# Layer 1's feed-forward part: down products written between block products, and the second half's operands made during the first half and kept in DRAM

## The chip, the cores and the metric

One core of a Trainium2 chip runs the whole program. The metric is the device time of one execution, in microseconds, and the time of a kernel is the median of its runs. Matrix products run on PE (TensorE) in float32; DVE (VectorE), ACT (ScalarE) and POOL (GpSimd) do the elementwise work; SP (SyncE) issues most DMAs, ACT a few. Each engine takes its own instructions strictly in their order, and waits at an instruction until what it needs is there.

## What is computed

The reference is a two-layer transformer block over 1024 latent tokens of width 1024 with a prefix of 256 context tokens. Layer 0 mixes tokens by a Fourier transform and windowed attention, layer 1 by neighbourhood attention over a 64-wide grid; each layer ends in a gated feed-forward part. Only layer 1's feed-forward part is touched, and in the last layer it covers the latent tokens alone:

```python
h = _rms(x, norm2_g[1]) * (1.0 + sc2) + sh2
x = x + g2 * ((silu(h @ wg) * (h @ wu)) @ wd)      # wg, wu: 1024 x 2816, wd: 2816 x 1024
```

## The kernel before

Every float32 operand of a product is split into a high and a low part of fewer bits, and each product is three matmuls: high x high, high x low, low x high (`mm3`, lines 74 to 76).

**Two halves.** Layer 1's feed-forward part runs over the tokens in two halves of 512 (`ci` 0 and 1), and in each over 22 tiles of 128 hidden columns, so over 44 tiles in all. `x` holds the residual stream for all tokens in SBUF.

**Block products ("p").** Gate and up projection of a tile are not multiplied out directly. The two weight blocks and the two halves of the contraction are combined so that 7 products of half size take the place of 8: `product7` (12 matmuls of 128x256 each) multiplies one of seven weight combinations (`t1` to `t4` are sums and differences of raw weight blocks, made on POOL at L1359) by one of seven operand combinations, held for the current half in `c_hi` and `c_lo`. `product` takes the seven results out of PSUM (`p_ps`, 3 buffers) into `p1`, `u2`, `u3`, `av`, `sg`, and at the end splits the tile's activation into `act_hi` (ACT) and `act_lo` (POOL).

**Weights of a block product.** `prepare1` and `parts_of` round a combination to `w_hi` (ACT, L1240), copy it into PSUM (`pmisc`, ACT, L1244, 2 buffers) and subtract it there on DVE to get `w_lo` (L1245); the seventh combination's `w_lo` is made on POOL. `w_hi` and `w_lo` have 6 buffers each.

**Down products ("d").** For each pair of tiles, 8 products of 6 matmuls of 128x512 (`down_product`) go to `d_ps` (PSUM, 3 buffers), and DVE adds each to `x` (L1437). The down weights are loaded as they are (`wd_raw`) and split by ACT (L1387) and POOL (L1388) into space of an earlier buffer, so that the trace shows them as `h_hi` and `h_lo`.

**Order.** The list `items` sets the order in this part, and PE, DVE, ACT and POOL take the instructions as written. Seven block products of a tile stand together, then four down products of the pair before; tiles 0 and 1 of each half have none, and each half ends with 4 + 8 down products in a row. Preparation runs up to 5 products ahead of use, and at most 7 items.

**Between the halves.** `norm1s(1)` normalises the second half during the first: 18 steps, four per tile from tile 1 on, the results stored to DRAM (`h_d`). At the end of the first half they are loaded back, and `combine` (16 half-width adds on POOL, 16 casts on ACT, 16 subtractions on DVE) makes `c_hi` and `c_lo` from them among the last down products.

Of the kernel before, what the change touches and what calls it, by code (L numbers as in the profile page):

```python
# [63 lines left out]
def build(tc, io):  # L64
# [1209 lines left out]
    def norm1s(ci, done):  # L1274


        ts = slice(ci * 512, ci * 512 + 512)
        ss = wk.tile([P, 512], F32, name="nrm_ss")
        for i, k in enumerate(reversed(range(KT))):
            if i == 0:  # L1280
                S.activation(ss, x[:, k, ts], AF.Square)
            else:
                sq = wk.tile([P, 512], F32, name="nrm_sq", **(dict(tag="nrm_r") if ci else dict(tag="t", bufs=4)))
                S.activation(sq, x[:, k, ts], AF.Square)
                G.tensor_tensor(ss, ss, sq, ALU.add)
            yield
        for r in norm_rstd(ss, 512, wk, ph):
            yield
        for i in range(4):
            both = []  # L1290
            for k in (i, i + 4):
                a, b = nA[3][:, k, 0:1], vec(1, 3)[:, k, 0:1]
                if ci:
                    h = wk.tile([P, 512], F32, name="nrm_h", tag="nrm_ss")
                    G.tensor_tensor(h, x[:, k, ts], r, ALU.mult)
                    S.activation(h, h, AF.Identity, bias=b, scale=a)
                    nc.scalar.dma_start(h_d[:, k], h)
                else:
                    t = wk.tile([P, 512], F32, name="nrm_t", tag="t", bufs=4)
                    V.scalar_tensor_tensor(t, x[:, k, ts], a, r, ALU.mult, ALU.mult)  # L1300
                    h = wk.tile([P, 512], F32, name="nrm_h", tag="wd", bufs=4)
                    S.activation(h, t, AF.Identity, bias=b, scale=1.0)
                both.append(h)
                yield
            if not ci:
                done(i, *both)
                yield
# [4 lines left out]
    def combine(i, h0, h4, tags=("act_hi", "act_lo")):  # L1312

        s, r = (wk.tile([P, 2, HT], F32, name="s_sum", tag=t, bufs=4) for t in tags)
# [16 lines left out]

    items = []
    for ci in range(2):
        for f in range(NF):
            items += [("p", ci, f, s) for s in range(7)]
            if f >= 2:
                items += [("d", ci, f // 2 * 2 - 2, dt) for dt in range(f % 2 * 4, f % 2 * 4 + 4)]
        items += [("d", ci, NF - 2, dt) for dt in range(KT)]
    products = [(n, i) for n, i in enumerate(items) if i[0] == "p"]
    LEAD_P, LEAD_I = 5, 7  # L1340
    tiles = {}

    def load_tile(n):

        if n < 2 * NF:
            f = n % NF
            tiles[n] = dict(b=[raw_half(io[w][1, f][:, i:i + 4])
                               for w, i in (("w_gate", 0), ("w_up", 0), ("w_up", 4), ("w_gate", 4))], w={})

    def prepare1(n, s):  # L1350

        if s == 0:
            load_tile(n + 1)
        d = tiles[n]
        b11, b12, b22, b21 = d["b"]

        def weight_sum(name, a, b):
            d[name] = wk.tile([P, 4, P], F32, name=name, tag="t", bufs=4)
            G.tensor_tensor(d[name], a, b, ALU.subtract)  # L1359

        if s == 0:
            weight_sum("t1", b12, b11)
            weight_sum("t2", b22, d["t1"])
        elif s == 1:
            weight_sum("t3", b22, b12)
        elif s == 3:
            weight_sum("t4", d["t2"], b21)
        src = (b11, d["t2"], d.get("t3"), d["t1"], d.get("t4"), b21, b22)[s]
        d["w"][s] = parts_of(src, G if s == 6 else V)
# [4 lines left out]
    h_d = tc.dram_tile([P, KT, 512], F32, name="h_d")  # L1374
    down_raw = {}

    def load_down(n):
        for h in range(2):
            raw = wk.tile([P, 4, P], F32, name="wd_raw", tag="wd", bufs=4)
            nc.sync.dma_start(raw, io["w_down"][1, n % NF][:, 4 * h:4 * h + 4])  # L1380
            down_raw[n, h] = raw

    def split_down(n, h):
        f = n % NF
        hi, lo = (w_room[f // 2 % 2][:, f % 2, h, t] for t in range(2))
        raw = down_raw.pop((n, h))
        S.copy(hi, raw)  # L1387
        G.tensor_tensor(lo, raw, fl(hi), ALU.subtract)  # L1388

    later = {}  # L1390

    def product(i, n, s):

        d = tiles[n]
        if s == 0:
            for name in ("p1", "u2", "u3", "sg"):
                d[name] = wk.tile([P, HT], F32, name=name)
            d["av"] = wk.tile([P, 2, HT], F32, name="av", bufs=2)
            d["act"] = [wk.tile([P, 512], F32R, name=m, bufs=4) for m in ("act_hi", "act_lo")]
        p1, u2, u3, sg, av, (hi, lo) = (d[k] for k in ("p1", "u2", "u3", "sg", "av", "act"))  # L1400
        ps = product7(d["w"].pop(s), (0, 4, 5, 3, 2, 1, 6)[s])
# [20 lines left out]
        else:  # L1422
# [3 lines left out]
            after(2, lambda: S.copy(hi, avf))  # L1426
            after(3, lambda: G.tensor_tensor(lo, avf, fl(hi), ALU.subtract))

    def down_product(ci, n, dt):
        f = n % NF  # L1430
        w_in = w_room[f // 2 % 2]
# [9 lines left out]
    own0 = norm1s(0, combine)  # L1441
# [5 lines left out]
    own1 = norm1s(1, None)  # L1447
    def first_tile():
        load_tile(0)
        for s in range(LEAD_P):  # L1450
            prepare1(0, s)
# [3 lines left out]
    done_p = LEAD_P  # L1455
    h_in = []
    with tc.manual_schedule(engines={E.PE, E.DVE, E.Activation, E.Pool}):
        now_p = 0
        for i, (kind, ci, f, s) in enumerate(items):
            n = ci * NF + f  # L1460
            while done_p < len(products) and done_p < now_p + LEAD_P + 1 and products[done_p][0] <= i + LEAD_I:
                _, pc, pf, ps_ = products[done_p][1]
                prepare1(pc * NF + pf, ps_)
                done_p += 1
            for step in later.pop(i, ()):
                step()
            if kind == "p":
                product(i, n, s)
                now_p += 1
                if s == 3:  # L1470
                    load_down(n)
                if f and s in (2, 5):
                    split_down(n - 1, s // 5)
            else:
                down_product(ci, n, s)
                last = i + 12 >= len(items) or items[min(i + 12, len(items) - 1)][1] > ci

                rest = sum(1 for it in items[i:i + 12] if it[0] == "d" and it[1] == ci) if last else 13
                if last and rest in (12, 10):
                    split_down(ci * NF + NF - 1, 0 if rest == 12 else 1)  # L1480
                if last and ci == 0 and rest in (11, 8, 5, 2):
                    j = (11 - rest) // 3
                    combine(j, *h_in[j], tags=("t", "t"))
            if ci == 0 and kind == "p" and f and s % 2 == 0:
                advance(own1, 1)
            if ci == 0 and kind == "p" and f == NF - 1 and s == 6:

                rooms = [dict(tag="nrm_ss"), dict(tag="nrm_r")], *([dict(tag="wd", bufs=4)] * 2,) * 3
                for k, room in enumerate(rooms):
# [121 lines left out]
```

## Time and profile before

| | |
|---|---|
| median of 3 runs | 2988.53 us (2986.49 to 2993.25) |
| the profiled execution's own time | 2990.69 us |
| its span in the trace | 2988.9 us |
| PE busy | 2821.1 us, 94% of the span |
| DVE, ACT, POOL busy | 51%, 41%, 27% |
| layer 1's feed-forward part | from 2198 us to the end |

The span runs from the first to the last instruction; the 1.8 us between it and the execution's own time lie around it. An idle time in the trace is put down to the event that came last before the engine went on, its releaser. `pmisc` and `p_ps` are PSUM buffers, `w_raw` and `wd_raw` raw weights.

### The profile page before, as it was taken

The page shows a single profiled execution, that of the slowest core. Times are in us where ns is not written, and L with a number is a line of the kernel's source. Part 1 is how long each engine was busy: PE and PEld are TensorE (multiplying, and loading weights), DVE is VectorE, ACT ScalarE, POOL GpSimd, SP SyncE. Part 2 cuts the span into 40 slices and gives each one's busy share as a digit, 9 for nine tenths or more (in the row PEclk, how much of TensorE's full clock was granted, in tenths as well). Part 3 has the DMA queues.
Part 4 walks back from the last instruction along what each step waited for, and adds up shares of the span by engine and source line. Part 5 has one row for each costly group of instructions (what it writes and reads, how often), then busy time and mean ns, then how long its engine had stood idle before and what let it go on. Part 6 is the DMA issues. An engine that isn't in the chain of part 4 may idle for free. (4 is left out here: it accounts for less than half of the span.)

```text
span 2988.9 us, 44472 instructions
## 1 busy us (share of the span) xinstructions
PE 2821.1 (94%) x16874; PEld 2352.6 (79%) x16874; DVE 1515.3 (51%) x3085; ACT 1212.9 (41%) x2402; POOL 810.4 (27%) x841
## 2 busy tenths in 40 slices
PE   7989999999999999999989999999986999889999
PEld 5876768888888888888767887777776888778888
DVE  5775553622323333333575242666464666656665
ACT  4345552511111111111353232666365666466664
POOL 1112332000000000000220003554155666656664
PEclk9989999999999999999999999999998999999999
DMA  7236664111011111011134236873542322332321
GB/s 273 81 119 232 213 213 139 57 43 36 29 50 43 36 36 43 29 43 43 56 113 144 84 103 173 192 180 86 170 136 86 110 95 99 103 106 96 99 97 68
DMA packets 154982, 310.60 MB, mean 104 GB/s; under 512 B 13424, under 2 KB 71280, under 8 KB 147728
## 3 DMA queue, kind: packets, MB, share of 16 engines
q1 hardware_dynamic: 146336, 288.80, 30.6%
q0 software_dynamic: 1952, 8.32, 1.0%
q10 hardware_dynamic: 6480, 10.63, 0.9%
q8 instruction: 133, 2.18, 0.3%
q14 instruction: 81, 0.66, 0.1%
HBM read 264.58 MB, written 43.12 MB: 103 GB/s over the span
## 5 line engine op out<-in xcount | busy, mean ns | idle before, releaser
L74 PE MATMUL p_ps<-c_hi,w_hi 128*128 128x256 f32 x1232 | 346.7, 281 | 17.5 <-DVE u L1414 7.3
L76 PE MATMUL p_ps<-c_hi,w_lo 128*128 128x256 f32 x1232 | 345.3, 280 | 2.0 <-DVE w_lo L1245 1.9
L75 PE MATMUL p_ps<-c_lo,w_hi 128*128 128x256 f32 x1232 | 345.5, 280 | 0.0
L810 POOL TENSOR_TENSOR nrm_ss<-nrm_ss,nrm_sq 128x512 f32<-128x512 f32 (+1 forms) x31 | 39.3, 1268 | 1013.2 <-PE d_ps L76 935.7
L775 ACT CAST w_hi<-w_raw 128x1024 fp32r<-128x1024 f32 x106 | 110.3, 1049 | 482.6 <-PE d_ps L75 270.5
L74 PEld LDWEIGHTS p_ps<-c_hi,w_hi 128*128 128x128 f32 x1232 | 236.4, 192 | 21.4 <-ACT pmisc L1244 6.9
L76 PEld LDWEIGHTS p_ps<-c_hi,w_lo 128*128 128x128 f32 x1232 | 236.1, 192 | 2.4 <-DVE w_lo L1245 2.4
L75 PEld LDWEIGHTS p_ps<-c_lo,w_hi 128*128 128x128 f32 x1232 | 236.1, 192 | 2.1 <-DVE c_lo L1322 0.2
L580 POOL TENSOR_SCALAR pr<-pr,st 128x640 f32<-128x640 f32 (+2 forms) x208 | 156.0, 751 | 267.4 <-DVE st L579 177.0
L878 DVE SCALAR_TENSOR_TENSOR x<-d_ps,mod,x 128x512 f32<-128x512 f32 (+1 forms) x240 | 157.4, 660 | 125.4 <-PE d_ps L76 125.4
L776 DVE TENSOR_TENSOR w_lo<-w_raw,w_hi 128x1024 fp32r<-128x1024 f32 x102 | 124.1, 1223 | 183.7 <-ACT w_hi L775 181.4
L862 DVE TENSOR_TENSOR sg<-sg,u_ps 128x512 f32<-128x512 f32 (+1 forms) x66 | 39.5, 598 | 320.2 <-PE u_ps L76 320.2
L1245 DVE TENSOR_TENSOR w_lo<-t,pmisc 128x512 fp32r<-128x512 f32 x176 | 119.7, 680 | 150.8 <-ACT pmisc L1244 145.3
L74 PE MATMUL d_ps<-act_hi,w_hi 128*128 128x512 f32 (+1 forms) x528 | 189.4, 359 | 3.4 <-DVE x L878 3.4
L75 PE MATMUL d_ps<-act_lo,w_hi 128*128 128x512 f32 (+1 forms) x528 | 189.2, 358 | 1.3 <-DVE act_lo L864 1.3
L76 PE MATMUL d_ps<-act_hi,w_lo 128*128 128x512 f32 (+1 forms) x528 | 189.3, 359 | 0.0
L74 PE MATMUL u_ps<-o_hi,w_hi 128*128 128x512 f32 (+1 forms) x528 | 188.4, 357 | 0.0
L76 PE MATMUL u_ps<-o_hi,w_lo 128*128 128x512 f32 (+1 forms) x528 | 188.4, 357 | 0.0
L75 PE MATMUL u_ps<-o_lo,w_hi 128*128 128x512 f32 (+1 forms) x528 | 188.4, 357 | 0.0
L74 PE MATMUL g_ps<-o_hi,w_hi 128*128 128x512 f32 (+1 forms) x528 | 188.4, 357 | 0.0
L76 PE MATMUL g_ps<-o_hi,w_lo 128*128 128x512 f32 (+1 forms) x528 | 188.3, 357 | 0.0
L75 PE MATMUL g_ps<-o_lo,w_hi 128*128 128x512 f32 (+1 forms) x528 | 188.3, 357 | 0.0
(328 smaller groups left out, 7478.7 us busy)
## 6 DMA issues: line engine op xcount, KB each, us to landing
ada_w<-ada_w SPq DMA_DIRECT2D x48, 1024.0 KB, 4.9
wd_raw<-w_down SPq DMA_DIRECT2D x88, 256.0 KB, 2.8
w_raw<-w_gate SPq DMA_DIRECT2D x88, 256.0 KB, 2.6
w_raw<-w_up SPq DMA_DIRECT2D x88, 256.0 KB, 2.7
k<-k_d SPq DMA_DIRECT2D x28, 640.0 KB, 10.3
w_raw<-w_in SPq DMA_DIRECT2D x24, 512.0 KB, 4.2
w_raw<-w_gate SPq DMA_DIRECT2D x22, 512.0 KB, 3.4
w_raw<-w_up SPq DMA_DIRECT2D x22, 512.0 KB, 3.5
```

The source lines that it names most:

```text
L74: TE.matmul(out, lh, rh, start=first, stop=False)
L75: TE.matmul(out, lh, rl, start=False, stop=False)
L76: TE.matmul(out, ll, rh, start=False, stop=last)
L580: G.tensor_scalar(self.pr[:, :n], self.pr[:, :n], st[:, 3:4], 0.0, ALU.mult, ALU.add)
L775: S.copy(hi, raw)
L776: eng.tensor_tensor(lo, raw, fl(hi), ALU.subtract)
L810: adder(i).tensor_tensor(ss, ss, sq, ALU.add)
L862: V.tensor_tensor(sg[:, :n], sg[:, :n], u_ps[:, :n], ALU.mult)
L878: V.scalar_tensor_tensor(xs, self.shaped(ps[:, :n]), vec(l, 5)[:, dt, v:v + 1], xs, ALU.mult, ALU.add)
L1245: eng.tensor_tensor(lo, src, first, ALU.subtract)
```

## The change

The feed-forward part's work is written in another order, and the second half's operands are made elsewhere:

- `items` puts the four down products of a tile after its third, fifth, sixth and seventh block product, one after each; for tile 22 (the first of the second half) all four stand after the second block product. Tiles now count through from 0 to 43, so that a pair's down products may fall into the next half.
- Preparation is three functions with fixed leads: `sums1` (POOL) 7 products ahead, `high1` (ACT) 5, `low1` 4.
- Splitting the down weights is four steps at four products of a tile, where it was two.
- `norm1s` makes the complete `c_hi` and `c_lo` of the second half during the first: normalise, combine, round, subtract, all on POOL and ACT, in 58 steps of which four stand in each tile from tile 1 on. It stores the parts to DRAM (`c_d`) with 32 DMAs issued by ACT. In tile 21, after each block product, two DMAs on SP load the operand that this product was the last to read. `combine` is used for the first half only.
- `act_hi` and `act_lo` have 3 buffers instead of 4, `wd_raw` has 3 of its own.

```diff
+    def norm1s():
...
+        for i in range(4):
+            h0, h4, s_, r_ = (wk.tile([P, 512], F32, name="own", bufs=4) for _ in range(4))
+            for k, h in ((i, h0), (i + 4, h4)):
+                G.tensor_tensor(h, x[:, k, 512:], r, ALU.mult)
+                S.activation(h, h, AF.Identity, bias=vec(1, 3)[:, k, 0:1], scale=nA[3][:, k, 0:1])
                 yield
+            G.tensor_tensor(s_[:, M1], h0[:, M2], h4[:, M2], ALU.add)
+            G.tensor_tensor(s_[:, M2], s_[:, M1], h0[:, M1], ALU.subtract)
+            yield
+            G.tensor_tensor(r_[:, M1], h0[:, M1], h0[:, M2], ALU.subtract)
+            G.tensor_tensor(r_[:, M2], h4[:, M1], s_[:, M2], ALU.subtract)
+            yield
+            for sl, src in ((slice(0, 1), h0[:, M1]), (slice(1, 3), h4), (slice(3, 5), s_), (slice(5, 7), r_)):
+                n = (sl.stop - sl.start) * HT
+                hi = wk.tile([P, 512], F32R, name="own_hi", tag="nrm_ss")
+                S.copy(hi[:, :n], src)
+                G.tensor_tensor(src.bitcast(F32R), src, fl(hi[:, :n]), ALU.subtract)
+                yield
+                for t, part in ((0, fl(hi[:, :n])), (1, src)):
+                    nc.scalar.dma_start(c_d[:, sl, t, i], part.rearrange("p (a n) -> p a n", n=HT))
+                yield
...
-    for ci in range(2):
-        for f in range(NF):
-            items += [("p", ci, f, s) for s in range(7)]
-            if f >= 2:
-                items += [("d", ci, f // 2 * 2 - 2, dt) for dt in range(f % 2 * 4, f % 2 * 4 + 4)]
-        items += [("d", ci, NF - 2, dt) for dt in range(KT)]
+    for n in range(NT1):
+        downs = [("d", n // 2 * 2 - 2, dt) for dt in range(n % 2 * 4, n % 2 * 4 + 4)] if n > 1 else []
+        where = (2, 4, 5, 6)
+        if n == NF:
+            where = (1, 1, 1, 1)
+        for s in range(7):
+            items.append(("p", n, s))
+            items += [d for d, w in zip(downs, where) if w == s]
+    items += [("d", NT1 - 2, dt) for dt in range(KT)]
...
-        for i, (kind, ci, f, s) in enumerate(items):
-            n = ci * NF + f
-            while done_p < len(products) and done_p < now_p + LEAD_P + 1 and products[done_p][0] <= i + LEAD_I:
-                _, pc, pf, ps_ = products[done_p][1]
-                prepare1(pc * NF + pf, ps_)
-                done_p += 1
+        for i, (kind, n, s) in enumerate(items):
             for step in later.pop(i, ()):
                 step()
...
+            q = 7 * n + s
+            sums1(q + LEAD + 2)
+            if q:
+                low1(q + LEAD - 1)
+            high1(q + LEAD)
+            product(i, n, s)
...
+            if 0 < n < NF - 1 and s in (0, 2, 4, 6):
                 advance(own1, 1)
-            if ci == 0 and kind == "p" and f == NF - 1 and s == 6:
...
+            if n == NF - 1:
 
+                for t, dst in ((0, c_hi), (1, c_lo)):
+                    nc.sync.dma_start(fl(dst[:, SLOTS[s]]), c_d[:, SLOTS[s], t])
```

What this makes of the engines' queues shows at three places.

DVE, one tile of the first half well after its start. Before, from the last block product's `u` on, all four additions to `x` stand behind it, with two further `w_lo` among them:

```order
L1419 TENSOR_TENSOR sg<-p_ps,p_22244 128x256
L1245 TENSOR_TENSOR w_lo<-t_22350,pmisc 128x512
L1421 TENSOR_TENSOR av<-av,u_22246 128x256
L1424 TENSOR_TENSOR u_22245<-p_ps,u_22245 128x256
L1245 TENSOR_TENSOR w_lo<-t_22326,pmisc 128x512
L1425 TENSOR_TENSOR av<-u_22245,sg 128x256
L1437 SCALAR_TENSOR_TENSOR x<-d_ps,mod_72,x 128x512
L1245 TENSOR_TENSOR w_lo<-t_22397,pmisc 128x512
L1437 SCALAR_TENSOR_TENSOR x<-d_ps,mod_72,x 128x512
L1245 TENSOR_TENSOR w_lo<-w_raw,pmisc 128x512
L1437 SCALAR_TENSOR_TENSOR x<-d_ps,mod_72,x 128x512 x2
```

DVE of the changed kernel, the same part of a tile:

```order
L1475 TENSOR_TENSOR u_22136<-u_22136,p_ps 128x256
L1505 SCALAR_TENSOR_TENSOR x<-d_ps,mod_72,x 128x512
L1425 TENSOR_TENSOR w_lo<-t_22178,pmisc 128x512
L1478 TENSOR_TENSOR sg<-p_ps,p_22134 128x256
L1480 TENSOR_TENSOR av<-av,u_22136 128x256
L1505 SCALAR_TENSOR_TENSOR x<-d_ps,mod_72,x 128x512
L1425 TENSOR_TENSOR w_lo<-t_22126,pmisc 128x512
L1483 TENSOR_TENSOR u_22135<-p_ps,u_22135 128x256
L1484 TENSOR_TENSOR av<-u_22135,sg 128x256
L1505 SCALAR_TENSOR_TENSOR x<-d_ps,mod_72,x 128x512
```

Each `x` now stands right behind the block product that its down product follows on PE, and one `w_lo` between two of them.

POOL, one tile of the first half while the second half is being normalised. Before (`nrm_h` is the second half's normalised operand, `h_lo` a split of down weights):

```order
L1359 TENSOR_TENSOR t_19590<-w_raw 128x512
L1359 TENSOR_TENSOR t_19592<-w_raw,t_19590 128x512
L1295 TENSOR_TENSOR nrm_h<-x,nrm_r 128x512
L1359 TENSOR_TENSOR t_19618<-w_raw 128x512
L1388 TENSOR_TENSOR h_lo<-wd_raw,h_lo 128x512
```

POOL of the changed kernel, one tile later (`own` holds the second half's operands, `own_hi` their high parts):

```order
L1340 TENSOR_TENSOR own<-own,own_hi 128x256
L1400 TENSOR_TENSOR t_19940<-w_raw 128x512
L1340 TENSOR_TENSOR own<-own,own_hi 128x512
L1492 TENSOR_TENSOR act_lo<-av,act_hi 128x512
L1400 TENSOR_TENSOR t_19971<-w_raw,t_19940 128x512
L1446 TENSOR_TENSOR h_hi<-wd_raw,h_hi 128x512
L1400 TENSOR_TENSOR t_19992<-w_raw 128x512
L1425 TENSOR_TENSOR w_lo<-w_raw,w_hi 128x512
```

The sums for the next tile now stand two products ahead of the cast that reads them, and subtractions for `own` have come between them.

SP at the turn of the halves. Before, the stored `h_d` comes back in eight loads behind the last weights of the first half:

```order
L1233 DMA w_raw<-h_d 128x512 x2
L1380 DMA wd_raw<-w_down 128x512
L1233 DMA w_raw<-h_d 128x512 x2
L1494 DMA h_in<-h_d 128x512 x2
L1380 DMA wd_raw<-w_down 128x512 x2
```

SP of the changed kernel, in tile 21:

```order
L1554 DMA c_lo<-c_d 128x1024
L1554 DMA c_hi<-c_d 128x1024 x2
L1554 DMA c_lo<-c_d 128x1024
L1233 DMA w_raw<-w_up 128x512
L1233 DMA w_raw<-w_gate 128x512
L1554 DMA c_hi<-c_d 128x1024
L1554 DMA c_lo<-c_d 128x1024
```

Fourteen loads of twice the size stand there now, the first two operands' ahead of two of the four weight loads of tile 23.

199 lines of the change are left out of this document (112 added, 87 removed).

## The prediction

> **What bounds the kernel now.** I read the share of PE first (94% of the span), then the busy times by stretch of the changed part, then the moment at which ACT takes each tile's first block product out of PSUM, which clocks the tiles, and last what PE waits for.
>
> ```profile
> span 2988.9 us, 44472 instructions
> PE 2821.1 (94%) x16874; PEld 2352.6 (79%) x16874; DVE 1515.3 (51%) x3085; ACT 1212.9 (41%) x2402; POOL 810.4 (27%) x841
> ...
> 2205.45:2331.59 126.14, 91.67 (x594) 84.12 (x595) 58.26 (x112) 76.90 (x138) 77.16 (x61) 0.86 0.29 97
> 2331.59:2575.07 243.48, 230.70 (x1622) 209.57 (x1621) 156.14 (x286) 151.56 (x286) 152.92 (x120) 1.00 0.30 98
> 2684.20:2960.16 275.96, 261.49 (x1838) 237.48 (x1837) 176.84 (x324) 171.81 (x323) 173.25 (x136) 1.00 0.28 92
> ...
> L74 PE MATMUL p_ps<-c_hi,w_hi x1232: 275/276/582, 2198.3 to 2967.8; 128*128 128x256 f32 x176
> ```
>
> The stretches give length, then busy time (and instructions) of PE, PE's weight loads, DVE, ACT and POOL, then granted clock, DMA share and GB/s. The last row is the first of a block product's three matmuls: the part begins at 2198.3. No engine but PE is busy for more than two thirds of a steady stretch, yet PE idles in all three. The tiles' clock, ACT's copy out of `p_ps`, for tiles 0, 6, 7, 21, 22, 26 and 43:
>
> ```profile
> 2205.45 0.36 ACT L1407 COPY p<-p_ps 128x256 f32<-128x256 f32 x1
> 2331.59 0.37 ACT L1407 COPY p<-p_ps 128x256 f32<-128x256 f32 x1 [1.99 <-PE p_ps L76]
> 2347.82 0.37 ACT L1407 COPY p<-p_ps 128x256 f32<-128x256 f32 x1 [1.99 <-PE p_ps L76]
> 2575.07 0.37 ACT L1407 COPY p<-p_ps 128x256 f32<-128x256 f32 x1 [1.99 <-PE p_ps L76]
> 2621.97 0.37 ACT L1407 COPY p<-p_ps 128x256 f32<-128x256 f32 x1 [1.96 <-PE p_ps L74]
> 2684.20 0.37 ACT L1407 COPY p<-p_ps 128x256 f32<-128x256 f32 x1 [1.99 <-PE p_ps L76]
> 2960.16 0.37 ACT L1407 COPY p<-p_ps 128x256 f32<-128x256 f32 x1 [1.99 <-PE p_ps L76]
> ```
>
> What PE's own work takes: a tile's seven block products, from their first matmul to the first down product, and two additions to `x` at the end, where DVE only follows PE:
>
> ```profile
> 2715.09 0.28 PE L74 MATMUL p_ps<-c_hi,w_hi 128*128 128x256 f32 x1
> 2724.62 0.39 PE L74 MATMUL d_ps<-act_hi,h_hi 128*128 128x512 f32 x1
> 2983.71 0.75 DVE L1437 SCALAR_TENSOR_TENSOR x<-d_ps,mod,x 128x512 f32<-128x512 f32 x1 [0.65 <-PE d_ps L76]
> 2985.11 0.75 DVE L1437 SCALAR_TENSOR_TENSOR x<-d_ps,mod,x 128x512 f32<-128x512 f32 x1 [0.65 <-PE d_ps L76]
> ```
>
> So a block product is 9.53 / 7 = 1.36 us, a down product 1.40, a full tile 9.53 + 4 x 1.40 = 15.13. A steady tile takes 2347.82 - 2331.59 = 16.23. Setting work against time:
>
> - Start, 2198.3 to 2331.59: 133.3 us for 6 tiles' block products, one more, and 16 down products, 80.9. Lost: **52.4**.
> - Steady, 15 + 17 tiles: 243.48 + 275.96 - 32 x 15.13. Lost: **35.3**.
> - Middle, 2575.07 to 2684.20: 109.1 us for 5 x 9.53 + 20 x 1.40 = 75.7. Lost: **33.5**.
> - End, from 2960.16: 28.7 us for 6 block and 12 down products, 25.0; the rest is the last addition and store, which stay.
>
> The work itself (308 block and 176 down products) does not change, so 121 us is all there is to gain.
>
> **The change, part by part. Steady tiles.** The loss is a burst on DVE. In one tile:
>
> ```profile
> 2708.39 0.39 PE L74 MATMUL d_ps<-act_hi,h_lo 128*128 128x512 f32 x1
> ...
> 2709.95 0.69 DVE L1245 TENSOR_TENSOR w_lo<-t,pmisc 128x512 fp32r<-128x512 f32 x1 [0.98 <-ACT pmisc L1244]
> 2710.55 1.06 DVE L1421 TENSOR_TENSOR av<-av,u 128x256 f32<-128x256 f32 x1
> 2712.46 0.41 DVE L1425 TENSOR_TENSOR av<-u,sg 128x256 f32<-128x256 f32 x1
> 2712.80 0.74 DVE L1437 SCALAR_TENSOR_TENSOR x<-d_ps,mod,x 128x512 f32<-128x512 f32 x1
> 2713.59 0.50 PE L74 MATMUL d_ps<-act_hi,h_lo 128*128 128x512 f32 x1 [0.85 <-DVE x L1437]
> ```
>
> PE needs a fourth `d_ps` buffer at 2708.39 + 3 x 1.40 = 2712.6; DVE, behind late `w_lo`s, frees the first at 2713.5. In the new order a down product stands alone between block products, at least 1.36 apart, so three buffers last over 8 us. DVE has 156.14 / 15 = 10.4 us of work in a tile of 15.13, ACT 10.1, POOL 10.2. The fullest place is the sixth product: 0.69 + 0.41 + 1.06 + 0.74 = 2.9 on DVE against 1.36 + 1.40 of PE, twice a tile, which the buffers take up. I take the loss to **0**; bounds 0 and the old 1.10 a tile.
>
> **Start.** Here the 18 steps that normalise the second half fall into tiles 1 to 5. From tile 0 to tile 6 the loss is 126.14 - 79.6 = 46.5, or 2.6 a step, and it comes out of the order, not out of load (POOL busy 77 of 126):
>
> ```profile
> 2247.72 0.69 DVE L1245 TENSOR_TENSOR w_lo<-t,pmisc 128x512 fp32r<-128x512 f32 x1 [6.10 <-ACT pmisc L1244]
> 2254.58 0.80 PE L74 MATMUL d_ps<-act_hi,h_hi 128*128 128x512 f32 x1 [7.35 <-DVE x L1437]
> 2205.87 0.38 PE L74 MATMUL p_ps<-c_hi,w_hi 128*128 128x256 f32 x1 [0.70 <-ACT p L1407]
> 2213.21 0.35 PE L74 MATMUL p_ps<-c_hi,w_hi 128*128 128x256 f32 x1 [2.97 <-DVE u L1414]
> 2226.10 1.28 POOL L1285 TENSOR_TENSOR nrm_ss<-nrm_ss,nrm_sq 128x512 f32<-128x512 f32 x1
> 2188.20 0.74 POOL L1318 TENSOR_TENSOR s_sum<-nrm_h,s_sum 128x256 f32<-128x256 f32 x1
> PE pmisc L164 <- POOL nrm_ss L1285: 2.7, 1, 2.7
> PE pmisc L170 <- DVE nrm_v L84: 1.4, 2, 1.1
> 2270.62 0.82 ACT L1296 ACTIVATE nrm_h<-nrm_h,mod,nA 128x512 f32<-128x512 f32 x1 [3.40 <-POOL nrm_h L1295]
> 2271.46 0.33 ACTq L1297 DMA_DIRECT2D h_d<-nrm_h  x1
> ```
>
> DVE stands 6.1 us before a `w_lo` for a later product, with `p_ps` and `d_ps` full behind it, since ACT waits for a sum on POOL that stands behind a step. Afterwards a sum stands two products ahead of ACT's cast, and that five ahead of PE: some 2.7 + 5.4 us of cover. What is left: the fourth product starting at 2205.87 instead of 2198.3 + 4.1 (3.5 us; the preparation ahead of it stays); POOL in tile 1, 8 ordinary operations and 3 sums of squares at 1.28, 14 us against PE's 9.5, a backlog of 4.5 that reaches PE partly (3); PE's own waits for the last sum of squares and for the reciprocal root (the two rows of `pmisc`, 4); the lower granted clock in these gaps (0.86 in the stretch's row; 2); tile 0's full PSUM buffers (2 of the 2.97). I keep **15** of the 52.4; bounds 6 (the first and half of `pmisc`'s waits) and the whole 52.4.
>
> Tiles 4 to 15 then carry the new steps. For each of 4 pairs of columns POOL does 2 products (1.28), 5 half-width (0.74) and 3 full subtractions (1.30, as `act_lo` takes below): 10.2 us in 12 steps, so 3.4 a tile, 13.7 with the ordinary 10.2, of 15.13. ACT's 8 x 0.82, 16 casts (0.62 below) and 32 x 0.33 to issue stores are 27 us in 12 tiles, 2.3 on top of 10.1. PE hides both; without that cover the rivals count. New waits: each of the 32 stores on ACT waits for POOL's subtraction, written two products before it; behind it on ACT stand `act_hi` and the next `w_hi`, which PE needs only four products later. A high part's buffer is written again two products after its store is issued:
>
> ```profile
> h_d<-nrm_h ACTq DMA_DIRECT2D x8, 256.0 KB, 2.0
> ```
>
> The same size landed in 2.0 us, less than two products, so I cost this at nothing.
>
> **Middle.** 12 down products in a row, `combine` between them and its aftermath are gone; DVE loses 16 subtractions there. In their place SP issues 14 loads in tile 21, each waiting for PE to have read the operand; behind them stand half of tile 23's weights. Up to the last operand's landing 14 x 0.524 MB, 1.0 of weights and 1.0 of output move, 9.4 MB, from the end of tile 21's first product; its reader, the last product of tile 22, starts 12 block and 8 down products later, 27.5 us. DMA rates in forty slices of the first 80 us, and of 1860 to 1980:
>
> ```profile
> GB/s 37 256 416 423 420 389 416 388 78 168 356 123 274 397 406 365 383 359 344 279 266 410 326 304 91 327 267 136 270 430 414 401 8 0 0 132 117 14 8 33
> GB/s 218 218 222 234 244 280 196 203 207 230 230 231 202 23 153 186 262 208 216 206 232 242 53 5 117 175 254 216 218 210 224 225 113 3 76 169 209 261 213 217
> ```
>
> At 400 GB/s 23.5 + 2.0 = 25.5, in time; at 210, where the loads filled 64 partitions each, 46.8, a wait of 19. These loads fill 128 partitions, like the first ones, so I take the upper rate. I keep **2** of the 33.5, for the first tiles of the half. The Trainium skill, "DMA: Bandwidth & Descriptors", section "Specifications", puts HBM's limit for a core at about 358 GB/s; by it the last operand would be 0.8 us late. The rows above it (416 to 430) don't show that limit.
>
> **End.** Only one down product, not four, now stands between tile 43's last block product and the first reader of its activation:
>
> ```profile
> 2968.56 0.41 DVE L1424 TENSOR_TENSOR u<-p_ps,u 128x256 f32<-128x256 f32 x1
> 2970.10 0.62 ACT L1426 CAST act_hi<-av 128x512 fp32r<-128x512 f32 x1 [1.76 <-DVE av L1425]
> 2970.80 1.30 POOL L1427 TENSOR_TENSOR act_lo<-av,act_hi 128x512 fp32r<-128x512 f32 x1 [1.01 <-ACT act_hi L1426]
> ```
>
> That chain took 3.5 us; PE has 1.40 + 4 x 0.23 before it needs `act_lo`: **+1**, at most 1.3.
>
> **Sum**, on the profiled execution's 2990.69: - 35.3 - (52.4 - 15) - (33.5 - 2) + 1 = 2887.5. That execution stood 2.2 above the median of 2988.53, so 2885 for a median.
>
> **The rivals.**
>
> - POOL becomes the bound while it makes the second half's operands. Steady POOL now waits some 6 of 16.2 us (152.92 busy of 243.48). If 3.5 of that stays as waits on ACT's casts, a tile takes 13.7 + 3.5 = 17.2, 2.1 more over 14.5 tiles: 30 us, **2915**. Against it: a late POOL finds its casts done. The Trainium skill, "GPSIMD Engine Reference", section "Engine selection", gives elementwise work to VectorE as about twice as fast; that speaks against these subtractions on POOL and for this rival, not for another price.
> - The loads come at 210 GB/s: 19 instead of 2, **2902**.
> - The steady tiles keep their 1.10, the change not doing what it says, if DVE stays late by ACT's chain: **2920**. Against it: the `x` no longer come in a burst.
> - Slower: ACT halts at a store until POOL has subtracted, POOL at a cast that stands behind the store, so a step costs 2.6 as before. 58 steps are 151 us in place of 46.5: **3027** by the median. It needs halts longer than PE's lead of 5 products, 6.8 us; from 1.9 us a step on, all gain is gone. For it: the 7.35 above. Against it: those were waits across two products, now there is cover.
>
> **How the numbers follow.** Forecast 0.65 (2870 to 2898: 6 to 28 lost at the start, 0 to 2 in the middle, and the runs' spread), POOL 0.17, slow loads 0.08, steady stall 0.05, slower 0.04; 0.01 for steps that just cost 1.9. The range takes the forecast, slow loads and POOL, 0.90: 2870 to 2917. About 0.2%, 6 us, is what a measurement here can tell from no change; faster by more 0.95, within 0.01, slower 0.04.
>
> **What would show it.** Copies of `p1` 15.1 apart in tiles 16 to 20 and 25 to 43; 15 to 16 in tiles 4 to 15 (17 is the POOL rival, 18 or more the slower one); PE waiting for `c_hi` or `c_lo` in tile 22 for under 2 us; granted clock near 1.00 from tile 3 on. I am wrong if PE still waits for `x` in most tiles, or for `w_lo` behind ACT's stores.

## The result, and the profile after

| | before | after |
|---|---|---|
| median | 2987.64 us (2986.49 to 2993.25, 4 runs) | 2900.19 us (2894.51 to 2901.23, 4 runs) |
| profiled execution, its span | 2990.69, 2988.9 us | 2901.23, 2899.4 us |
| ratio | | 0.970, 95% interval 0.968 to 0.972 |

The change is worth 87 us. The page's first rows of the changed kernel, to be held against those of before:

```profile
span 2899.4 us, 44678 instructions
PE 2799.8 (97%) x16874; PEld 2346.2 (81%) x16874; DVE 1510.4 (52%) x3069; ACT 1214.7 (42%) x2402; POOL 825.3 (28%) x857
```

PE has the same 16874 matmuls and is busy for 97% of a shorter span. The windows of the part, cut at copies of `p1` (tiles 0 to 16, 17 to 21, 22 to 24, 25 to 42, and from tile 43 on; columns as in the prediction), and the first matmul of the block products:

```profile
2202.52:2476.39 273.87, 254.69 (x1782) 234.72 (x1783) 183.14 (x320) 195.04 (x364) 220.63 (x182) 0.98 0.39 127
2476.39:2551.98 75.59, 75.59 (x542) 70.42 (x541) 51.26 (x95) 51.22 (x95) 50.37 (x41) 1.00 0.45 152
2551.98:2597.34 45.36, 45.36 (x326) 42.22 (x325) 32.41 (x57) 30.22 (x58) 30.46 (x25) 1.00 0.68 235
2597.34:2869.50 272.16, 272.16 (x1946) 253.54 (x1945) 184.51 (x342) 184.52 (x343) 180.23 (x144) 1.00 0.31 100
2869.50:2899.40 29.90, 25.18 (x144) 21.28 (x142) 13.34 (x22) 3.90 (x9) 6.61 (x6) 0.98 0.18 71
...
L74 PE MATMUL p_ps<-c_hi,w_hi x1232: 276/276/415, 2196.3 to 2881.3; 128*128 128x256 f32 x176
```

From tile 17 to tile 43 length and PE's busy time are one number: 75.59 / 5, 45.36 / 3 and 272.16 / 18 are all 15.12, a full tile's work. The steady loss and that of the middle are gone. What is left lies in tiles 0 to 16, where the steps that make the second half's operands run: from 2196.3 to 2476.39 are 280.1 us, for 17 tiles' block products, one more, and 15 x 4 down products, 247.4. Lost: 32.7. What PE waits for in the whole part:

```profile
PE d_ps L75 <- POOL act_lo L1492: 12.8, 7, 4.0
PE d_ps L74 <- ACT act_hi L1489: 2.0, 1, 2.0
PE pmisc L1320 <- DVE w_lo L1425: 1.8, 1, 1.8
PE p_ps L74 <- ACT own L1328: 1.5, 2, 1.3
```

(Sum of the waits in us, their number, the longest.) The largest is for `act_lo`, at a down product that is the first to read a new pair of activations. The longest but one of these, in tile 6, with what ACT and POOL did just ahead of it:

```profile
2298.67 0.62 ACT L1489 CAST act_hi<-av 128x512 fp32r<-128x512 f32 x1 [4.00 <-DVE av L1484]
...
2301.15 0.62 ACT L1339 CAST own_hi<-own 128x512 fp32r<-128x512 f32 x1
2301.84 1.27 POOL L1340 TENSOR_TENSOR own<-own,own_hi 128x512 fp32r<-128x512 f32 x1 [5.67 <-ACT own_hi L1339]
2303.07 1.27 POOL L1492 TENSOR_TENSOR act_lo<-av,act_hi 128x512 fp32r<-128x512 f32 x1
2304.40 0.80 PE L75 MATMUL d_ps<-act_lo,h_hi 128*128 128x512 f32 x1 [3.60 <-POOL act_lo L1492]
```

Read from the bottom: PE waits 3.60 for `act_lo`. POOL makes it late because the instruction ahead of it, a step's subtraction, stood 5.67 us for the cast `own_hi`. ACT reaches that cast only as its fifth operation behind `act_hi`, and `act_hi` itself came 4.00 late, behind a single slow DVE operation that the last section shows; so this is the clearest of the waits, not the usual one (the four others in tiles 4 to 16 are 0.5 to 1.6). `act_lo` could have begun when `act_hi` was done, at 2299.29; it began 3.8 us later, on an engine that had been idle until 2301.84. In the whole part POOL waited like this seven times:

```profile
POOL own L1340 <- ACT own_hi L1339: 25.8, 7, 5.7
```

The theory I took to the runs has three parts: the steady gain comes from standing the downs apart (rival: from the fixed leads of the preparation); the rest of the loss is `act_lo` behind a step on POOL (rivals: POOL's load as such, and ACT's halts at the stores); the norm's sums of squares on POOL are a second cause in tiles 1 to 3.

### The profile page after: what moved, and what is told of

Read it like the earlier page. It is cut to its first block, busy times and chain, and to the rows that moved or that the text cites. A ratio compares the mean times of both kernels' runs of the same rounds, so it can differ in the third digit from the quotient of the medians.

```text
span 2899.4 us, 44678 instructions
## 1 busy us (share of the span) xinstructions
PE 2799.8 (97%) x16874; PEld 2346.2 (81%) x16874; DVE 1510.4 (52%) x3069; ACT 1214.7 (42%) x2402; POOL 825.3 (28%) x857
## 3 DMA queue, kind: packets, MB, share of 16 engines
HBM read 269.83 MB, written 48.37 MB: 110 GB/s over the span
## 5 line engine op out<-in xcount | busy, mean ns | idle before, releaser
L1505 DVE SCALAR_TENSOR_TENSOR x<-d_ps,mod,x 128x512 f32<-128x512 f32 x176 | 132.1, 751 | 127.0 <-PE d_ps L76 126.4
```

Of the source, the lines that this page charges most:

```text
L1505: V.scalar_tensor_tensor(x[:, dt, ts], ps, vec(1, 5)[:, dt, 0:1], x[:, dt, ts], ALU.mult, ALU.add)
```

## The experiments

The place at which the part begins differs between profiles by more than some edits are worth (first product at 2196.3 here, at 2204.0 in another kernel that is no different up to there). So beside the medians stand lengths between copies of `p1`, from one profile of each kernel, in us:

| kernel | median | tiles 1 to 3 | tiles 4 to 16 | tiles 0 to 21 |
|---|---|---|---|---|
| the changed kernel | 2900.19 | 54.27 | 209.23 | 349.46 |
| downs together | 2919.02 | 53.92 | 218.58 | 358.45 |
| no steps, no loads | 2878.25 | 40.94 | 196.56 | 323.46 |
| `act_lo` one item earlier | 2897.24 | 57.50 | 199.68 | 343.13 |
| no stores, no loads | 2898.20 | 53.93 | 202.99 | 342.88 |
| three steps a tile | 2889.65 | 50.33 | 197.32 | 332.17 |
| low parts on DVE | 2889.55 | 53.98 | 196.36 | 336.30 |
| sums of squares on DVE | 2894.09 | 49.05 | 205.17 | 340.18 |
| the last three together | 2881.79 | 48.37 | 196.86 | 330.21 |
| the same, `act_lo` earlier | 2884.07 | 49.54 | 197.87 | 331.54 |

### Where the steady gain comes from

**The downs together again**, everything else as in the changed kernel:

```diff
-        where = (2, 4, 5, 6)
-        if n == NF:
-            where = (1, 1, 1, 1)
+        where = (6, 6, 6, 6)
```

> The changed kernel with the four down products of a tile all behind its seventh block product again; everything else stays new (leads of the preparation, the second half's operands by way of DRAM). If the steady gain comes from standing the down products apart: tiles 25 to 43 go back to about 16.2 us each, tiles 17 to 22 too, and act_lo, which now has no block product's time to be late in, is waited for more; the kernel takes some 35 to 50 us more than the changed one (2935 to 2950). If it comes from the preparation's new fixed leads instead: these tiles stay at 15.1 and the time within 6 us of 2900.

Measured: 2919.02 us (ratio to before 0.976, 0.975 to 0.978). Seventeen steady tiles, 25 to 41, by window, and what ACT and DVE waited for there:

```profile
2616.95:2873.99 257.04, 257.04 (x1838) 238.78 (x1837) 173.49 (x324) 172.05 (x323) 171.58 (x135) 1.00 0.34 103
```

```profile
DVE w_lo L1423 <- ACT pmisc L1415: 4.7, 8, 0.6
...
ACT w_hi L1411 <- POOL t L1398: 5.2, 8, 0.7
```

257.04 / 17 is 15.12. Four downs in a row cost a steady tile nothing, so my theory of the steady gain falls. Standing apart is worth something elsewhere: 9.4 us in tiles 4 to 16, where the steps run, and 3.4 at the turn. The other 6 to 7 us of the median lie ahead of the part, which began 7.1 us later in this profile (2203.4). The edit changes nothing there, so I don't count them to it; why the part began later is not shown.

**The downs apart, alone, in the kernel before:**

```diff
-            items += [("p", ci, f, s) for s in range(7)]
-            if f >= 2:
-                items += [("d", ci, f // 2 * 2 - 2, dt) for dt in ...]
+            where = (6, 6, 6, 6) if f == NF - 1 else (2, 4, 5, 6)
+            for s in range(7):
+                items.append(("p", ci, f, s))
+                items += [d for d, w in zip(downs, where) if w == s]
```

> The kernel before with only the down products stood among the block products (behind the third, fifth, sixth and seventh; the last tile of each half keeps them together), its preparation, its norm steps and its middle as they were. If standing them apart ends the steady loss: tiles 7 to 20 and 27 to 42 take 15.1 instead of 16.2 and the kernel takes 2950 to 2960. If the steady gain comes only from the preparation's new order, which this kernel lacks: they stay at 16 or more, and the time within 8 us of 2990. The kernel with the downs together again has shown 15.12 with the new preparation, so either the two edits each suffice or only the second does.

Measured: 2970.67 us, ratio 0.994 (0.992 to 0.995): neither number. The steady tile went from 16.23 to 16.02. Over sixteen of them, 26 to 41, PE and ACT waited for:

```profile
PE d_ps L76 <- POOL h_hi L1390: 6.1, 4, 1.5
PE d_ps L76 <- POOL h_lo L1390: 5.2, 4, 1.5
...
ACT w_hi L1240 <- POOL t L1361: 83.7, 32, 4.1
```

The wait for `x` that I had named is gone, as forecast, and a new one of nearly its size stands in its place: the first down product now comes earlier in the tile, and POOL's split of its weights doesn't. Was that the only thing in the way? **The same, with the split two products earlier:**

```diff
-                if f and s in (2, 5):
-                    split_down(n - 1, s // 5)
+                if f and s in (0, 3):
+                    split_down(n - 1, s // 3)
```

> The kernel before with the down products stood apart, and the split of the down weights two products earlier (at the first and fourth block product instead of the third and sixth), so that POOL's low part is no longer later than its reader. If standing the downs apart does end the old stall and only this split hid it: tiles 26 to 42 take 15.1 to 15.3 instead of 16.02, and the kernel about 27 us less than with them apart alone (2940 to 2950). If the late weight parts themselves are the limit: 15.8 or more.

Measured: 2990.91 us, ratio 1.0003 (0.9994 to 1.0012), steady tiles at 16.6 to 17.4. PE's and POOL's waits over 16 tiles:

```profile
PE d_ps L75 <- POOL act_lo L1429: 14.1, 8, 1.9
...
POOL h_hi L1390 <- ACT h_hi L1389: 52.3, 8, 6.8
```

With the split out of the way the next wait is `act_lo`, behind a POOL that halts up to 6.8 us at ACT's cast. Three orders in the old preparation, and each has a stall of 0.9 us or more a tile, of which only the name changes. That points at the preparation. Its clearest trace in the kernel before are these rows, over tiles 26 to 42:

```profile
PE d_ps L74 <- DVE x L1437: 14.5, 17, 0.9
...
DVE w_lo L1245 <- ACT pmisc L1244: 44.9, 34, 1.7
...
ACT w_hi L1240 <- POOL t L1359: 61.4, 17, 3.6
```

ACT waits 3.6 a tile for a weight sum that POOL was given one product ahead of the cast. So the last run took **only the sums' lead** out of the kernel with the downs together:

```diff
-        for q in range(LEAD + 2):
+        for q in range(LEAD):
             sums1(q)
...
-            sums1(q + LEAD + 2)
+            sums1(q + LEAD)
```

> The changed kernel with the down products together, and with each weight sum on POOL written right ahead of ACT's cast of it, no longer two products ahead. In the kernel before ACT waited 61.4 us for these sums in 17 steady tiles (3.6 a tile) and DVE 44.9 for the copies behind them; with the downs together and the sums two products ahead 5.2 and 4.7, at 15.12 a tile. If the sums' lead is what ended the steady stall: tiles 25 to 42 go to 15.8 to 16.5, and the kernel takes 15 to 40 us more than with the downs together alone (2935 to 2960). If it is the rest of the new order (the low parts one product later, the down weights' split in four separate places): they stay within 0.2 of 15.12.

Measured: 2977.47 us, ratio 0.996 (0.995 to 0.997), 58 us more than with the downs together alone, where I had expected 15 to 40; the steady tiles went where I had said. Seventeen steady tiles, 25 to 41, and the waits in them:

```profile
2658.15:2930.40 272.25, 261.45 (x1838) 237.45 (x1837) 172.91 (x324) 170.55 (x323) 172.87 (x136) 1.00 0.31 98
```

```profile
PE d_ps L74 <- DVE x L1503: 10.8, 17, 0.6
...
DVE w_lo L1423 <- ACT pmisc L1415: 54.1, 34, 2.5
...
ACT w_hi L1411 <- POOL t L1398: 59.4, 17, 3.5
```

272.25 / 17 is 16.01, and the old chain is back row by row: ACT at POOL's sum (59.4, before 61.4), DVE at ACT's copy (54.1, before 44.9), PE at `x` (10.8, before 14.5). The busy times of DVE, ACT and POOL are those of the fast version within 2 us. A lead of two products, on one engine, for operations that take 1.3 us each, is worth 0.90 us a tile, of the 1.10 that the kernel before lost. It isn't quite the old preparation: there three of a tile's four sums stood one product ahead of their casts and one three products, here three stand right ahead and one three. Over the whole stretch from tile 0 to tile 43 it is 742.56 - 679.39 = 63.2 us, 40.2 of it in tiles 0 to 16.

That gives one way through the 87.7 us by which the stretch from tile 0's to tile 43's `p1` became shorter (754.71 to 666.98): 63.2 the sums' lead, 12.4 the downs apart, 12.1 everything else in the new order. Those 12.1 hold a gain of 25.7 at the turn (tiles 21 to 24: 92.88 before, 67.20 in this last run), 0.21 in each of 22 steady tiles, and a loss of 18.3 in tiles 0 to 16 (304.69 before, 323.03 here), where 58 steps without that lead stand in place of 18. Since this run has less lead than the kernel before, the 63.2 prices two products against none, and the shares may come out differently in another sequence.

### What is left at the start

**No steps and no loads** (the 58 steps and the 14 loads are left out; the second half is computed with the first half's operands):

```diff
-            if 0 < n < NF - 1 and s in (0, 2, 4, 6):
+            if False:
...
-                for t, dst in ((0, c_hi), (1, c_lo)):
-                    nc.sync.dma_start(fl(dst[:, SLOTS[s]]), c_d[:, SLOTS[s], t])
+                pass
```

> The changed kernel without the 58 steps that make the second half's operands and without the loads that fetch them; the second half is computed with the first half's operands. It prices all the steps together. If the loss of 32.7 us in tiles 0 to 16 comes from the steps (by whichever path), what is left there is the lead-in and the clock, 6 to 10 us, and the kernel takes 2874 to 2880. If the loss belongs to the start itself (a throttled clock, the weights' first loads), 25 or more of the 32.7 stay and the time is above 2890. Tile 22 and the rest of the part stay at 15.12 by both.

Measured: 2878.25 us. From the first product to the end of tile 16 only 7.0 of the 32.7 us stay: the loss is the steps', as the first theory had it. Every tile from 3 on takes 15.12 or stands in the same turn of 45.36. The steps cost 26.0 us by the last column: 13.3 in tiles 1 to 3, 12.7 in tiles 4 to 16. The loads cost nothing, since tiles 22 to 24 take 45.36 with and without them. Tiles 4 to 16 with no step, in the changed kernel, and with `act_lo` earlier (next run), as windows:

```profile
2254.56:2451.12 196.56, 196.56 (x1406) 183.16 (x1405) 133.22 (x247) 133.34 (x249) 131.07 (x105) 1.00 0.34 105
```

```profile
2267.16:2476.39 209.23, 199.75 (x1404) 184.15 (x1404) 144.87 (x247) 143.53 (x271) 168.94 (x141) 0.99 0.41 134
```

```profile
2271.33:2471.01 199.68, 198.73 (x1406) 183.84 (x1405) 136.88 (x247) 143.42 (x271) 169.87 (x143) 1.00 0.45 140
```

**`act_lo` one item earlier**, ahead of the next tile's first step:

```diff
-            after(3 if n < NT1 - 1 else 2, act_low)
+            after(2, act_low)
```

> The changed kernel with act_lo made one item earlier, right behind act_hi and ahead of the next tile's first own step on POOL. If act_lo's short lead behind that step is what holds PE in tiles 4 to 16: PE's wait for act_lo (12.8 us in 7 waits) falls under 3 us, and the kernel takes 8 to 14 us less (2886 to 2892). If POOL's load as such is the bound, the wait turns up elsewhere (for w_lo or p_ps) and the time stays within 4 us of 2900.

Measured: 2897.24 us, a median 3 us lower, which these runs don't tell from none. PE's waits for `act_lo` fell from 12.8 to 2.7, as the theory said, but the time didn't follow by as much. In tiles 4 to 16 it did: 9.6 of 12.7 us gone, with POOL as busy as before (169.87 of 199.68 us, 85%), so load as such isn't the bound there. In tiles 1 to 3 the kernel lost 3.2 more, with new waits, at the norm's matmuls and at a `w_lo`:

```profile
PE pmisc L1320 <- DVE w_lo L1425: 4.9, 1, 4.9
PE p_ps L76 <- POOL w_lo L1425: 2.9, 2, 2.7
```

**No stores and no loads** (arithmetic of the steps kept; again the second half uses the first half's operands):

```diff
-                for t, part in ((0, fl(hi[:, :n])), (1, src)):
-                    nc.scalar.dma_start(c_d[:, sl, t, i], ...)
+                pass
```

> The changed kernel without the 32 stores of the second half's operands on ACT and without the 14 loads that fetch them; the arithmetic of the steps stays, the second half is computed with the first half's operands. If ACT's halts at the stores (each waits for POOL's subtraction) carry the loss in tiles 4 to 16: it falls by 10 us or more and the kernel takes 2885 to 2890. If POOL's order carries it: it falls by under 4 us, 2896 to 2900.

Measured: 2898.20 us, a median no different, but 6.2 less in tiles 4 to 16: between the two theories. Of the 6.2, 5.1 lie in tiles 5 to 7 (51.73 in the changed kernel, 46.68 here). There the changed kernel's profile has the one slow DVE operation that the last section shows, 4.24 us, and this one has none above 1.6. POOL still halted at the casts:

```profile
POOL own L1340 <- ACT own_hi L1339: 21.3, 8, 5.1
```

So the stores aren't the root of the loss, and what they add to it is not shown: most of the 6.2 may be that one operation's. A warning on releasers belongs here. In the changed kernel ACT's wait for a `w_hi` is put down to a store's DMA; without any store the same wait, of the same 2.26 us, at the same place in tile 5, is put down to PE. The first fence is the changed kernel, the second the one without stores:

```profile
2287.41 0.63 ACT L1413 CAST w_hi<-t 128x512 fp32r<-128x512 f32 x1 [2.26 <-DMA c_d<-own]
```

```profile
2291.05 0.62 ACT L1412 CAST w_hi<-t 128x512 fp32r<-128x512 f32 x1 [2.26 <-PE p_ps L75]
```

**Three steps a tile, none at the first block product:**

```diff
-            if 0 < n < NF - 1 and s in (0, 2, 4, 6):
+            if 0 < n < NF - 1 and s in (2, 4, 6):
```

> The changed kernel with three of the second half's steps in a tile instead of four: none behind the first block product, the rest at the third, fifth and seventh, so that they last until tile 20. If a step at the first product is what delays act_lo: tiles 4 to 20 lose under 4 us instead of 12.7, and tile 2 and 3 lose less (11 steps of the norm are spread over four tiles, not three); tiles 0 to 20 take 10 to 16 us less than in the changed kernel. If the number of steps sets the loss, whatever their place: the same loss, over more tiles, the time within 4 us of 2900.

Measured: 2889.65 us (ratio 0.967, 0.965 to 0.968), 17.3 us less by the last column. From tile 4 to the end of the steps in tile 20:

```profile
2270.87:2527.23 256.36, 255.52 (x1822) 237.96 (x1823) 182.29 (x323) 187.95 (x350) 212.90 (x177) 1.00 0.42 134
```

256.36 for 17 tiles is 15.08 each: the steps are free, with POOL 83% busy, where it was 81% busy in tiles 4 to 16 of the changed kernel. Place and rate within a tile decide, not the load; this run changes both and doesn't part them.

**The low parts on DVE, and the sums of squares on DVE,** one edit for each run:

```diff
-                G.tensor_tensor(src.bitcast(F32R), src, fl(hi[:, :n]), ALU.subtract)
+                V.tensor_tensor(src.bitcast(F32R), src, fl(hi[:, :n]), ALU.subtract)
```

> The changed kernel with the low parts of the second half's operands subtracted on DVE instead of POOL (16 subtractions, 12 of them full width at 1.30 us on POOL). If POOL's load and the halts behind it carry the loss: tiles 4 to 16 lose 5 to 9 us less. If it is ACT's order (own_hi behind the copy of p1, the store behind own_hi): the halt moves to DVE, where it is ahead of the additions that free PSUM, and the loss stays or grows, 2898 to 2910.

```diff
-                G.tensor_tensor(ss, ss, sq, ALU.add)
+                V.tensor_tensor(ss, ss, sq, ALU.add)
```

> The changed kernel with the seven additions of the norm's squares on DVE instead of POOL; nothing else. Tiles 1 to 3 take 54.3 us in the changed kernel, 40.9 without any step. If POOL's backlog from these additions is what holds PE there: tiles 1 to 3 take 46 to 49. If PE's own waits for the norm (its matmuls for the sum and the reciprocal root) hold it: 52 or more.

Measured: 2889.55 us (0.967, 0.965 to 0.969) and 2894.09 (0.968, 0.967 to 0.969). With the low parts off POOL tiles 4 to 16 take 196.36, as with no step at all, more than the 5 to 9 us I had given: the subtractions on POOL, by their halts or their time, were the whole of that loss, and by the run with `act_lo` earlier 9.6 of it went by way of `act_lo`. DVE now stands at those casts instead (12.2 us), and PE waits for nothing in these tiles. With the sums off POOL tiles 1 to 3 take 49.05, 5.2 less, a hair above what I gave for POOL's backlog. Their windows, changed kernel first:

```profile
2212.89:2267.16 54.27, 45.27 (x300) 41.07 (x299) 29.52 (x56) 41.36 (x77) 42.95 (x35) 0.91 0.27 88
```

```profile
2214.49:2263.54 49.05, 42.62 (x298) 39.05 (x297) 35.88 (x64) 41.36 (x76) 34.84 (x27) 0.97 0.31 97
```

About half of the 5.2 is clock: PE's busy time for the same work fell from 45.27 to 42.62, as the granted clock rose from 0.91 to 0.97.

**The three together, and with `act_lo` earlier as well:**

> The changed kernel with three edits that each helped alone: three steps of the second half in a tile instead of four (-17.3 us from tile 0 to tile 22, by the copies of p1), the low parts on DVE (-13.2) and the sums of squares on DVE (-9.3). Without any step that stretch takes 323.5 us, in the changed kernel 349.5. If all three act on one chain, POOL's order and ACT's behind it, the gains overlap down to a floor: 324 to 329 us there, and the kernel takes 2878 to 2886. If DVE, with 23 operations more, now holds PSUM: 332 or more, and the time is no better than with three steps alone (2889.65).

> The kernel with the three edits (three steps, low parts and sums on DVE), and act_lo one item earlier. If act_lo's short lead is still a wait of its own there: 1 to 4 us less than with the three edits alone. If the lead mattered only behind a step of the second half on POOL, which is gone now: within 1 us of it, or slower by up to 2, as the cast and the subtraction now stand ahead of the next weights' sums.

Measured: 2881.79 us (2881.73 to 2883.31; ratio 0.964, 0.963 to 0.965) and 2884.07 (0.965, 0.963 to 0.966). The first is faster than the changed kernel, whose interval, 0.968 to 0.972, lies apart, and it leaves nothing out. Its 330.21 in the last column is 1.2 above my band and 6.8 above no steps at all; the gains overlap (17.3, 13.2 and 9.3 alone, 19.3 together), as one chain would have them, but as they also must where only 26.0 can be lost. `act_lo` earlier adds nothing that can be told from zero once no step halts in front of it.

## Why the prediction was right, and where it wasn't

2885 was forecast, 2900 measured, inside 2870 to 2917 and 2 us above the likeliest case's own range, whose top was 2898. The sign and most of the size were right; that the miss is no larger is partly luck, since the part began 2.0 us earlier and the middle cost 2 less than reckoned. By its steps:

- **Steady: 0 forecast, 0 measured, for a reason that was half right.** The burst on DVE behind late `w_lo`s was the stall. That "a down product stands alone between block products", so that three buffers last, is true and not what ended it: with the downs together the tile is also 15.12, and with them apart in the old preparation it is 16.02. What ended it is that "a sum stands two products ahead of ACT's cast", which I had written down for the start alone.
- **Start: 15 forecast, 32.7 measured; this is the mis-sized term.** The lead-in with tile 0 was right: 3.5 + 2 forecast, 16.6 - 10.9 = 5.7 measured. Tiles 1 to 3: 9 forecast (backlog 3, `pmisc` 4, clock 2), 54.27 - 39.8 = 14.5 measured, with 2.0 of waits at `pmisc`, 7.1 at `act_lo`, `act_hi` and smaller ones, and 45.27 - 39.8 = 5.5 more busy time than work, the clock at 0.91. Tiles 4 to 16: nothing forecast, 209.23 - 13 x 15.13 = 12.5 measured. PE's waits there are 8.0 for `act_lo` and 1.5 put down to a step's activation on ACT; the rest is busy time above the work, 199.75 against 196.56, at a clock of 0.99. Tiles 5 to 7, which hold the slow DVE operation, lose 6.4, the next two rounds of three tiles 3.2 and 2.6.
- **The step that failed** is "PE hides both", with "act_hi and the next w_hi, which PE needs only four products later" as its cover. I counted leads for the weights and none for `act_lo`. It stands on POOL behind the step of the next tile's first block product, and PE wants it two products after that; the step waits for a cast that ACT takes up only five operations after `act_hi`, the one thing that `act_lo` needs. Moving the step (at a lower rate), moving `act_lo`, or taking the subtraction off POOL each removed 9.6 to 12.9 of the 12.7 us.
- **The POOL rival** (2915, 30 us) had the right engine and the right kind of wait, POOL halted at ACT's casts, at 1.0 a tile over 13 tiles rather than 2.1 over 14.5. "A late POOL finds its casts done" was the argument against it, and POOL's 25.8 us at `own_hi` answer that. But it isn't POOL as the bound: 83 to 85% busy, it cost little or nothing in another order.
- **Middle: 2 forecast, 0 measured.** The assumed 400 GB/s held for most of the loads' time. DMA rates in the 40 slices of the 30 us from 2536, when the loads run:

```profile
GB/s 11 0 115 268 410 410 366 208 218 339 328 388 358 412 393 421 410 421 421 410 415 399 407 391 399 407 407 410 393 412 355 352 341 366 410 399 396 322 254 240
```

  Of the 40 slices 22 lie between 390 and 421, above the 358 that the Trainium skill gives as a core's limit ("DMA: Bandwidth & Descriptors", section "Specifications"), and PE waited for no operand. That the operands from DRAM, and not only the absent burst of `combine`, made the turn short wasn't tried apart.
- **End: +1 forecast, 29.90 - 28.7 = +1.2 measured.** The first block product came 2.0 earlier than before, which I had not counted; by the other profiles of changed kernels (2195.6 to 2204.0) that is within what this place varies. Start +17.7, middle -2, end +0.2 and these -2.0 make 13.9, of the 13.7 us by which the profiled execution (2901.23) lay above the 2887.5 of the sum.
- **The slower case** needed 2.6 us on every step, or 1.9 to use up the gain. They came to 26.0 / 58 = 0.45.

Of what I had named as signs, copies 15.1 apart in tiles 17 to 20 and 25 to 43 and no wait for `c_hi` or `c_lo` were there (tile 16 was 14.73, catching up). Two were not: 15 to 16 in tiles 4 to 15, where single tiles took 12.8 to 19.6, and a clock near 1.00 from tile 3 on, where tile 3 had 0.92. Of the two signs of being wrong neither came: PE waited for no `x`, and for no `w_lo` behind ACT's stores.

## What to carry to other kernels

When an engine makes an operand for the next one, compare at each hand-over how far ahead the maker's instruction stands in its queue: two products of lead for the weight sums on POOL, against none, were worth 63 us here, and a better order of the products themselves 12. When steps are slipped into free time, don't add up busy shares; list, for each step that can halt, what stands behind it on its engine and which of those has the shortest lead to its reader. And when a moved stall comes back under another name, as it did twice here, look one engine further up the chain.

## What the hardware showed that I had not expected

One DVE operation with both inputs in SBUF took ten times its usual time. First the group, then the operation between the first and the last of the ten POOL operations that ran back to back around it:

```profile
L1480 DVE TENSOR_TENSOR av<-av,u x44: 415/416/4235, 2209.2 to 2879.4; 128x256 f32<-128x256 f32 x44
```

```profile
2283.56 1.30 POOL L1340 TENSOR_TENSOR own<-own,own_hi 128x512 fp32r<-128x512 f32 x1 [5.04 <-ACT own_hi L1339]
...
2292.22 4.24 DVE L1480 TENSOR_TENSOR av<-av,u 128x256 f32<-128x256 f32 x1
...
2294.87 1.31 POOL L1400 TENSOR_TENSOR t<-w_raw 128x512 f32<-128x512 f32 x1
```

It ended at 2296.46, 0.28 after POOL fell idle, having outlasted three POOL operations; the `act_hi` that waits for it, shown above, came 4.00 late, and so did the chain behind it in tile 6. The Trainium skill, "SBUF — State Buffer", section "SBUF: two separate sides", has such a DVE operation and one of GpSimd lock each other out for a whole instruction; the row fits that, and shows a loser passed over for several. It was the one such case in this trace, and no run isolated it.

The same page's lock shows again, more plainly, in the run with the low parts on DVE. The full-width low part took 1.20 us in the mean on DVE, with both inputs in SBUF, and 1.33 on POOL, while a `w_lo` with one input in PSUM takes 0.68. The low part's group on DVE first, from the run with low parts there, then on POOL and the `w_lo`, in the changed kernel:

```profile
L1340 DVE TENSOR_TENSOR own<-own,own_hi 128x512 fp32r<-128x512 f32 x12 | 14.4, 1203 | 12.2 <-ACT own_hi L1339 12.2
```

```profile
L1340 POOL TENSOR_TENSOR own<-own,own_hi 128x512 fp32r<-128x512 f32 x12 | 15.9, 1328 | 28.2 <-ACT own_hi L1339 25.8 <-DVE u L1468 2.4
...
L1425 DVE TENSOR_TENSOR w_lo<-t,pmisc 128x512 fp32r<-128x512 f32 x176 | 119.3, 678 | 12.4 <-ACT pmisc L1417 7.8 <-POOL t L1400 4.3 <-issue 0.2
```

The mean of 1.20 hides two kinds. Six of the twelve took 0.69, and the POOL operation that began then took about 1.8 in place of 1.3. The other six took 1.28 to 1.84 and ended some 0.55 after the POOL operation that they met, while the POOL operation behind that one took 1.75. One of each kind, from the run with low parts on DVE:

```profile
2300.13 0.69 DVE L1340 TENSOR_TENSOR own<-own,own_hi 128x512 fp32r<-128x512 f32 x1 [1.47 <-ACT own_hi L1339]
2300.18 1.79 POOL L1446 TENSOR_TENSOR h_hi<-wd_raw,h_hi 128x512 fp32r<-128x512 f32 x1
...
2336.17 1.30 POOL L1446 TENSOR_TENSOR h_hi<-wd_raw,h_hi 128x512 fp32r<-128x512 f32 x1
2336.18 1.83 DVE L1340 TENSOR_TENSOR own<-own,own_hi 128x512 fp32r<-128x512 f32 x1
2337.42 1.75 POOL L1400 TENSOR_TENSOR t<-w_raw 128x512 f32<-128x512 f32 x1
```

The factor of two that the page "GPSIMD Engine Reference", section "Engine selection", of the Trainium skill gives for such work shows in the six that went first (0.69 against 1.33), and not in the mean; the gain of those runs came from what no longer stood in POOL's queue.
